# Weight loads of a four-stage hybrid decoder layer issued from GpSimd's queue instead of SyncE's

## The chip, the cores and the metric

One core of a Trainium2 chip runs the whole kernel in one launch. The metric is the device time of one execution in microseconds (us); lower is better. The engines are named as the profile names them: PE (TensorE, matmuls), PEld (TensorE's weight loads), DVE (VectorE), ACT (ScalarE), POOL (GpSimd), SP (SyncE, which here only issues DMAs; its rows are marked SPq).

## The reference, cut to what matters

One layer of a decoder is applied to 1024 prompt tokens and to 8 x 4 sample tokens, 1056 tokens in all, everything in float32:

```
h = rmsnorm(x);  z = h @ w_in                       # 1024 -> 6432 columns
u = z_c[:512] * sigmoid(z_c[512:]);  c = silu(layernorm(dwconv31(u)));  ya = c @ w_conv_out
r,k,v,decay,alr,gate = token-shifted z_r (+ small LoRA products)
S_t = S_{t-1} diag(w_t) + (S_{t-1} a_t) b_t^T + v_t k_t^T;  y_t = S_t r_t       # 16 heads of 64
yb = groupnorm(y) ... @ w_rw_out
x = x + (sig(g1)*ya + sig(g2)*yb) @ w_mix_out
up = rmsnorm(x) @ w_up;  f = gelu(dwconv3(up)[:3072]) * dwconv3(up)[3072:];  x = x + f @ w_down
```

The outputs are the two normalised results and the new states.

## The kernel before, in words

**Weights.** Every large product is done as three matmuls in a reduced float format (`mm3`, L69 to L73): the high part of the weights with the high part of the activations, the high part with the low part, and the low part with the high part. So each weight tile is split before use, in `wjob` (L41 to L51), `wjob2` (L1572 to L1582) and `ffn_last` (L1589 to L1595), always in three steps: a DMA brings the tile `wraw` (L47, L1579, L1593; 128 partitions with up to 8 runs of 512 bytes each, 512 KB), ACT rounds it to `whi` (L48), and POOL subtracts to get `wlo` (L49). There are 155 such loads. `wraw` has one buffer up to the end of the convolution's output product (pool `wraw`, L110) and two after that (pool `wraw2`, L120); `whi` and `wlo` have two each (L108). A new load may start when the `wlo` of the load before has been computed, since that is the last reader of the buffer; the next `whi` may be written when the product that used the buffer two tiles ago is done.

**Stages.** The work goes through five stretches. (1) Start (to about 63 us): nine token tiles are loaded, normalised and transposed into `hH` and `hL`; parameter rows are loaded (`consts`, L158 to L170) and transposed (`turn`, L172). (2) Convolution (to about 317 us): products for the gated convolution input and for the LoRA inputs, while DVE does 31 taps per channel tile (L359). (3) Recurrence (to about 1395 us, `mixer_b`): 16 blocks of 256 tokens go through `prep` (L885), `stage` (L992), `combine` (L1061), `chain` (L1089) and `group_norm` (L1159), and the remaining products of `w_in` (`rkv_tile`, `gate`) are woven between as filler. In `prep` POOL builds `BK` (L982, L983) and scales `alr` (L957). In `stage` POOL masks `LQ` and `E` (L1011), SP stores and reloads pieces of `LQ` (L1019, L1021), DVE inverts small triangles (L1028, L1030), and the result goes out and back (L1034, L1038). The order of these streams is written by a small planner (`drive`, L701) that keeps its own matmul clock; it knows nothing of DMAs. (4) Convolution output (to about 1458 us): `conv_out` (L432), per tile one half-size weight load, a load of `ga` (L438), a product of 36 matmuls and a store `d_ma` (L443); at the same time 1 MB pieces of the recurrence's result are loaded into `hL` (L819). (5) Tail (to the end): `merge`, `mix`, and the gated MLP (`ffn_up`, `ffn_down`, `ffn_last`), 72 or 54 matmuls per weight tile.

**Queues.** All DMAs go through SP's queue in order, but for eight small parameter rows that POOL issues in `consts` (L168, groups 1 to 3). An instruction that waits at the head of a queue holds all behind it. Within each engine a scheduler orders the instructions from the order in which the code emits them and from its own estimate of their durations.

Of the kernel before, what the change touches and what calls it, by code (L numbers as in the profile page):

```python
# [31 lines left out]
class Net:  # L32
# [8 lines left out]
    def wjob(self, src, nk=8, lo_eng=None):  # L41
        nc = self.nc
        m = src.shape[-1]
        raw = self.rp.tile([128, 8, 128], F32, tag="wraw", name="wraw")
        hi = self.wp.tile([128, 8, 128], F32R, tag="whi", name="whi")
        lo = self.wp.tile([128, 8, 128], F32R, tag="wlo", name="wlo")
        nc.sync.dma_start(out=raw[:, :nk, :m], in_=src.rearrange("(k p) c -> p k c", p=128))  # L47
        nc.scalar.activation(out=hi[:, :nk, :m], in_=raw[:, :nk, :m], func=AF.Copy)  # L48
        (lo_eng or nc.gpsimd).tensor_tensor(  # L49
            out=lo[:, :nk, :m], in0=raw[:, :nk, :m], in1=hi[:, :nk, :m].bitcast(F32), op=ALU.subtract)  # L50
        return hi, lo  # L51
# [1520 lines left out]
    def wjob2(self, src, nk, lo_eng=None):  # L1572
        nc = self.nc
        m = src.shape[-1]
        v = lambda t: t.rearrange("p a b -> p (a b)")[:, :nk * m].rearrange("p (k c) -> p k c", c=m)
        raw = v(self.rp.tile([128, 8, 128], F32, tag="wraw", name="wraw"))
        hi = v(self.wp.tile([128, 8, 128], F32R, tag="whi", name="whi"))
        lo = v(self.wp.tile([128, 8, 128], F32R, tag="wlo", name="wlo"))
        nc.sync.dma_start(out=raw, in_=src.rearrange("(k p) c -> p k c", p=128))  # L1579
        nc.scalar.activation(out=hi, in_=raw, func=AF.Copy)  # L1580
        (lo_eng or nc.gpsimd).tensor_tensor(out=lo, in0=raw, in1=hi.bitcast(F32), op=ALU.subtract)
        return hi, lo  # L1582

    def ffn_last(self, g, f, acc, room):

        nc, a, G = self.nc, self.a, self.G
        rows = a["w_down"][0][g * G * 128:(g + 1) * G * 128]
        wh, wl = (t[:, 0:G, 0:D] for t in room)
        for h in range(4):  # L1589
            raw = self.rp.tile([128, 8, 128], F32, tag="wraw", name="wraw")  # L1590
            raw = raw.rearrange("p a b -> p (a b)")[:, :G * 256].rearrange("p (k c) -> p k c", c=256)
            c = slice(h * 256, (h + 1) * 256)
            nc.sync.dma_start(out=raw, in_=rows[:, c].rearrange("(k p) c -> p k c", p=128))  # L1593
            nc.scalar.activation(out=wh[:, :, c], in_=raw, func=AF.Copy)
            nc.gpsimd.tensor_tensor(out=wl[:, :, c], in0=raw, in1=wh[:, :, c].bitcast(F32), op=ALU.subtract)  # L1595
        with ExitStack() as e:
            xp = self.pool(e, "fin", 2)
            last = None
            for t0, t1 in ((0, 3), (3, 6), (6, 9)):
                toks = self.TOK[t0:t1]  # L1600
                c0 = toks[0][0]
                w = sum(n for _, n in toks)
                s = slice(c0, c0 + w)
                ssum = xp.tile([128, 384], F32, tag="ssum", name="ssum")
                for i in range(ND):
                    c = slice(i * 128, (i + 1) * 128)
                    ps = self.pm.tile([128, 512], F32, tag="mm", name="mm")
                    for k in range(G):
                        self.mm3(ps[:, :w], (wh[:, k, c], wl[:, k, c]), (f[k][0][:, s], f[k][1][:, s]), k == 0, k == G - 1)
                    x = acc[i][:, s]  # L1610
                    nc.vector.tensor_tensor(out=x, in0=ps[:, :w], in1=x, op=ALU.add)
                    if i == 0:
                        nc.scalar.activation(out=ssum[:, :w], in_=x, func=AF.Square)
                    else:
                        sq = xp.tile([128, 384], F32, tag="sq", name="sq")
                        nc.scalar.activation(out=sq[:, :w], in_=x, func=AF.Square)
                        nc.gpsimd.tensor_tensor(out=ssum[:, :w], in0=ssum[:, :w], in1=sq[:, :w], op=ALU.add)
                    nc.scalar.activation(out=x, in_=x, func=AF.Copy, scale=self.col("norm_final_g", i))
                    if last and i % 2:
                        next(last, None)  # L1620
                last = self.final(xp, acc, toks, ssum)
            self.run(last)
# [59 lines left out]
```

## Time and profile before

| | us |
|---|---|
| median of 3 runs | 2564.65 |
| lowest, highest of 3 runs | 2553.85, 2574.9 |
| the profiled execution | 2538.03 |
| its span, from the first to the last instruction | 2536.3 |

The profile is of one execution, with every instruction's start and length. Busy time is the time in which an engine ran at least one instruction. A wait is the idle time of an engine just before an instruction, put down to what released it. The granted clock is the rate at which PE was allowed to run, as a share of full speed. The chain of work that ended last is followed back from the last instruction. A DMA's own row on SP or POOL is the time of its issue, not of its transfer.

### The profile page before, as it was taken

The numbers are of one execution on the slowest core, as the hardware profiler recorded it, in microseconds if no ns is written. First come the engines' busy times: TensorE is split into PE (matmuls) and PEld (weight loads), VectorE is DVE, ScalarE is ACT, GpSimd is POOL, SyncE is SP. The second block draws the span as 40 slices with busy tenths as digits, with TensorE's granted clock in tenths as the row PEclk, the third lists the DMA queues.
The fourth block names the chain that finished last, engine by engine and source line by source line (L and its number), as shares of the span: only waits on it lengthen the run. The fifth ranks groups of instructions, "written<-read, shape, count | busy, mean of one in ns | idle before, by whom it ended". The sixth has DMA issues, their size and how long they took to land.

```text
span 2536.3 us, 41660 instructions
## 1 busy us (share of the span) xinstructions
PE 2367.6 (93%) x16094; PEld 2140.9 (84%) x16094; DVE 1427.9 (56%) x3588; ACT 918.7 (36%) x1748; POOL 909.1 (36%) x879
## 2 busy tenths in 40 slices
PE   5889989999788799999989999999999999999998
PEld 4878888777676677777777899999999999999998
DVE  5799955586646674555464434465444534445345
ACT  4133433354244354454434322333222222223125
POOL 3332253244324443443333243433323323323333
PEclk9899987898688698999779999999999999999999
DMA  3223443243233333533323854431111111111111
GB/s 104 56 60 130 171 149 89 81 121 93 78 89 79 93 107 83 140 98 94 94 64 96 273 178 131 128 128 44 44 47 48 44 51 44 47 48 41 54 46 75
DMA packets 307640, 230.64 MB, mean 91 GB/s; under 512 B 90492, under 2 KB 287123, under 8 KB 306921
## 3 DMA queue, kind: packets, MB, share of 16 engines
q1 hardware_dynamic: 307185, 227.80, 31.1%
q8 instruction: 127, 2.08, 0.4%
q14 instruction: 72, 0.59, 0.1%
q0 software_dynamic: 256, 0.17, 0.0%
HBM read 157.45 MB, written 70.45 MB: 90 GB/s over the span
## 4 chain that ended last, share of the span: by engine, by line
PE 66%; DVE 7%; DMA 7%; POOL 3%; issue 2%; ACT 1%; SPq 1%; POOLq 0%; DVEq 0%; ACTq 0%
PE mm L54 52%; PE w L54 7%; DMA L<-dL 4%; PE c L54 2%; PE y L54 2%; PE w L61 2%; DVE tm L1028 1%; DVE x L1030 1%; DVE t L961 1%; DMA ga<-d_ga 0%; POOL BK L982 0%; POOL wlo L49 0%; POOL LQ L1011 0%; DVE lnQ L666 0%; DVE v L486 0%
## 5 line engine op out<-in xcount | busy, mean ns | idle before, releaser
L54 PE MATMUL mm<-hH,whi 128*128 128x352 f32 (+1 forms) x2568 | 887.6, 346 | 27.0 <-DVE bcol L496 11.2
L54 PE MATMUL mm<-hL,whi 128*128 128x352 f32 (+1 forms) x2568 | 866.2, 337 | 0.2 <-DVE hL L248 0.2
L54 PE MATMUL mm<-hH,wlo 128*128 128x352 f32 (+1 forms) x2568 | 862.7, 336 | 0.0
L54 PEld LDWEIGHTS mm<-hH,whi 128*128 128x128 f32 (+1 forms) x2568 | 499.4, 194 | 55.9 <-issue 14.1
L54 PEld LDWEIGHTS mm<-hL,whi 128*128 128x128 f32 (+1 forms) x2568 | 500.9, 195 | 11.2 <-DVE hL L248 0.5
L54 PEld LDWEIGHTS mm<-hH,wlo 128*128 128x128 f32 (+1 forms) x2568 | 500.6, 195 | 8.7 <-issue 0.2
L49 POOL TENSOR_TENSOR wlo<-wraw,whi 128x1024 fp32r<-128x1024 f32 (+2 forms) x123 | 292.5, 2378 | 462.0 <-ACT whi L48 427.9
L48 ACT ACTIVATE whi<-wraw 128x1024 fp32r<-128x1024 f32 (+2 forms) x123 | 126.0, 1025 | 366.8 <-PE mm L54 270.1
L1544 DVE SCALAR_TENSOR_TENSOR c<-u,par,c 128x1024 f32<-128x1024 f32 x96 | 167.0, 1739 | 55.6 <-ACT c L1540 55.6
L359 DVE SCALAR_TENSOR_TENSOR sg<-cu,par,sg 128x1024 f32<-128x1024 f32 x120 | 185.1, 1550 | 3.4 <-ACT sg L357 1.7
L1514 DVE TENSOR_TENSOR u<-mm,rs 128x352 f32<-128x352 f32 x144 | 73.2, 509 | 186.5 <-PE mm L54 186.3
L54 PE MATMUL mm<-fH,whi 128*128 128x352 f32 x504 | 163.4, 324 | 0.0
L1569 DVE TENSOR_TENSOR acc<-mm,acc 128x352 f32<-128x352 f32 x168 | 86.8, 523 | 135.0 <-PE mm L54 135.0
L54 PE MATMUL mm<-fH,wlo 128*128 128x352 f32 x504 | 162.7, 323 | 0.0
L54 PE MATMUL mm<-fL,whi 128*128 128x352 f32 x504 | 162.7, 323 | 0.0
L1028 DVE TENSOR_TENSOR tm<-L,x 128x60 f32<-128x60 f32 (+24 forms) x496 | 99.4, 200 | 79.7 <-DMA L<-dL 72.5
L1030 DVE TENSOR_TENSOR x<-x,tm 128x60 f32<-128x60 f32 (+24 forms) x496 | 105.0, 212 | 7.0
L1525 POOL COPY lr<-u 128x2 f32<-128x2 f32 x48 | 9.0, 187 | 276.3 <-DVE u L1514 267.6
L54 PE MATMUL w<-E,BK 64*128 64x128 f32 x512 | 90.7, 337 | 8.8 <-DVE tm L1028 3.4
L1011 POOL TENSOR_SCALAR_AFFINE_SELECT LQ<-LQ 64x512 f32<-64x512 f32 x64 | 44.1, 690 | 148.3 <-ACT LQ L1007 146.8
L54 PEld LDWEIGHTS mm<-fH,whi 128*128 128x128 f32 x504 | 94.8, 188 | 0.5
L54 PEld LDWEIGHTS mm<-fH,wlo 128*128 128x128 f32 x504 | 95.0, 188 | 0.0
(379 smaller groups left out, 3971.2 us busy)
## 6 DMA issues: line engine op xcount, KB each, us to landing
wraw<-w_in SPq DMA_DIRECT2D x50, 512.0 KB
wraw<-w_up SPq DMA_DIRECT2D x48, 512.0 KB
wraw<-w_down SPq DMA_DIRECT2D x32, 384.0 KB
L<-dL SPq DMA_DIRECT2D x16, 512.0 KB
d_alr<-la SPq DMA_DIRECT2D x8, 528.0 KB
d_cum<-lc SPq DMA_DIRECT2D x8, 528.0 KB
d_gout<-lg SPq DMA_DIRECT2D x8, 528.0 KB
d_k<-k SPq DMA_DIRECT2D x8, 528.0 KB
```

The source lines that it names most:

```text
L48: nc.scalar.activation(out=hi[:, :nk, :m], in_=raw[:, :nk, :m], func=AF.Copy)
L49: (lo_eng or nc.gpsimd).tensor_tensor(out=lo[:, :nk, :m], in0=raw[:, :nk, :m], in1=hi[:, :nk, :m].bitcast(F32), op=ALU.subtract)
L54: self.nc.tensor.matmul(out, l, r, start=start, stop=stop)
L61: self.nc.tensor.transpose(out, x, ident)
L359: nc.vector.scalar_tensor_tensor(out=c[:, 0:TP], in0=u[:, t:t + TP], scalar=self.col("conv_w", t * 4 + i), in1=c[:, 0:TP], op0=ALU.mult, o ...
L961: nc.vector.scalar_tensor_tensor(out=t1[:, u], in0=r[:, u], scalar=self.col("r_k", 2 * J + u), in1=km[:, u], op0=ALU.mult, op1=ALU.mult)
L1011: nc.gpsimd.affine_select(out=w, in_=w, pattern=[[0, 4], [1, 2], [1, 64]], compare_op=ALU.is_ge, fill=0.0, base=-1, channel_multiplier=-1)
L1028: nc.vector.tensor_tensor(out=tm[:, :a, :m], in0=L[:, s:s + 1, s + 1:32].to_broadcast([128, a, m]), in1=X[:, :a, s:s + 1].to_broadcast([12 ...
L1030: nc.vector.tensor_tensor(out=X[:, :a, s + 1:32], in0=X[:, :a, s + 1:32], in1=tm[:, :a, :m], op=ALU.add)
L1514: nc.vector.tensor_tensor(out=u[:, 2 + t0:2 + t0 + m], in0=p, in1=rs[:, t0:t0 + m], op=ALU.mult)
L1544: nc.vector.scalar_tensor_tensor(out=c[:, 0:TP], in0=u[:, t:t + TP], scalar=wt, in1=c[:, 0:TP], op0=ALU.mult, op1=ALU.add)
L1569: nc.vector.tensor_tensor(out=acc[i][:, s], in0=ps[:, :BW], in1=acc[i][:, s], op=ALU.add)
```

## The change

The three statements that load weights are issued from POOL's queue in place of SP's; nothing else is edited.

```diff
@@ wjob @@
-        nc.sync.dma_start(out=raw[:, :nk, :m], in_=src.rearrange("(k p) c -> p k c", p=128))
+        nc.gpsimd.dma_start(out=raw[:, :nk, :m], in_=src.rearrange("(k p) c -> p k c", p=128))
@@ wjob2 @@
-        nc.sync.dma_start(out=raw, in_=src.rearrange("(k p) c -> p k c", p=128))
+        nc.gpsimd.dma_start(out=raw, in_=src.rearrange("(k p) c -> p k c", p=128))
@@ ffn_last @@
-            nc.sync.dma_start(out=raw, in_=rows[:, c].rearrange("(k p) c -> p k c", p=128))
+            nc.gpsimd.dma_start(out=raw, in_=rows[:, c].rearrange("(k p) c -> p k c", p=128))
```

All 155 loads move, and the scheduler orders the other instructions somewhat differently around them. On POOL at the start, where the first load stands at the head of the queue, this is the difference (+ is the changed kernel):

```order
+L49 TENSOR_TENSOR wlo<-wraw,whi 128x1024
 L165 MEMSET st 128x128
 L168 DMA st<-conv_dw_w 124x128
-L128 ISA
-L128 AFFINE_SELECT ident<-ident 128x128
 L168 DMA st<-conv_dw_b 4x128
 L168 DMA st<-conv_ln_g 4x128
 L168 DMA st<-conv_ln_b 4x128
-L49 TENSOR_TENSOR wlo<-wraw,whi 128x1024
 L168 DMA st<-ffn_dw_b 48x128
 L168 DMA st<-ffn_dw_w 48x128 x3
+L47 DMA wraw<-w_in 128x8x128
```

The first `wlo` now stands ahead of the memset of the parameter tile `st` and of POOL's parameter loads, and the second weight load stands behind them.

On POOL where the recurrence begins (the first `prep`: `P`, `PC`, `BK` and `alr` are its tiles), before:

```order
L49 TENSOR_TENSOR wlo<-wraw,whi 128x1024 x2
L903 MEMSET P 128x8
L906 COPY PC<-P 128x8
L982 TENSOR_TENSOR BK<-kn,cum 64x8x64 x2
L49 TENSOR_TENSOR wlo<-wraw,whi 128x1024
L957 TENSOR_TENSOR alr<-alr,k 128x512
L983 TENSOR_TENSOR BK<-alr,cum 64x8x64 x2
```

and in the changed kernel, same engine and place:

```order
L49 TENSOR_TENSOR wlo<-wraw,whi 128x1024
L47 DMA wraw<-w_in 128x8x128
L49 TENSOR_TENSOR wlo<-wraw,whi 128x1024
L47 DMA wraw<-w_in 128x8x128
L903 MEMSET P 128x8
L906 COPY PC<-P 128x8
L982 TENSOR_TENSOR BK<-kn,cum 64x8x64 x2
L49 TENSOR_TENSOR wlo<-wraw,whi 128x1024
L957 TENSOR_TENSOR alr<-alr,k 128x512
L47 DMA wraw<-w_in 128x8x128
L983 TENSOR_TENSOR BK<-alr,cum 64x8x64 x2
```

Each load follows the `wlo` that frees its buffer, here between `alr` and the second pair of `BK`. In the whole recurrence 8 loads stand right ahead of a mask of L1011 and 2 right ahead of a `BK`.

On SP in the convolution output (`hL` are the 1 MB pieces of the recurrence's result, `d_ma` the stores of the stage's product), the difference:

```order
-L47 DMA wraw<-w_conv_out 128x4x128
 L819 DMA hL<-d_y_426 128x2112
+L819 DMA hL<-d_y_427 128x2112
 L443 DMA d_ma_401<-ga 128x1056
-L47 DMA wraw<-w_conv_out 128x4x128
-L819 DMA hL<-d_y_427 128x2112
+L819 DMA hL<-d_y_428 128x2112
+L443 DMA d_ma_402<-ga 128x1056
 L438 DMA ga<-d_ga_411 128x1056
```

The weight loads are gone from between the `hL` loads, and the third `hL` load now stands ahead of the first `d_ma` store.

## Rows read from the trace of the kernel before

**Rows 1.** The page: busy time, share of the span and instructions of PE and POOL, and the granted clock of PE in 40 equal slices (tenths).
```profile
PE 2367.6 (93%) x16094; PEld 2140.9 (84%) x16094; DVE 1427.9 (56%) x3588; ACT 918.7 (36%) x1748; POOL 909.1 (36%) x879
...
PEclk9899987898688698999779999999999999999999
```

**Rows 2.** Busy time of each engine by stage (start, convolution, recurrence, convolution output, tail): stretch, its length, then per engine the busy us and instructions, then the granted clock, the DMA engines' share and GB/s.
```profile
0.00:63.40 63.40, 35.24 (x181) 27.24 (x182) 34.48 (x107) 29.36 (x50) 19.40 (x47) 0.92 0.34 104
63.40:317.00 253.60, 235.44 (x1283) 208.38 (x1283) 234.49 (x234) 87.80 (x151) 78.46 (x48) 0.95 0.32 104
317.00:1395.00 1078.00, 970.04 (x7620) 799.51 (x7619) 634.46 (x2379) 471.73 (x1068) 423.88 (x443) 0.85 0.37 97
1395.00:1458.40 63.40, 57.33 (x357) 55.15 (x358) 28.64 (x50) 23.49 (x33) 16.00 (x12) 0.97 0.84 273
1458.40:2536.30 1077.90, 1069.52 (x6663) 1050.66 (x6661) 495.81 (x818) 306.33 (x446) 371.37 (x331) 1.00 0.23 70
```

**Rows 3.** The page: the chain of work that ended last, share of the span by engine (a q marks an engine's queue, issuing or waiting).
```profile
PE 66%; DVE 7%; DMA 7%; POOL 3%; issue 2%; ACT 1%; SPq 1%; POOLq 0%; DVEq 0%; ACTq 0%
```

**Rows 4.** What SP's queue waited for, whole span: instruction, releaser, us in total, times, longest.
```profile
SPq L47 <- POOL wlo L49: 531.9, 81, 17.9
```

**Rows 5.** The same for the recurrence alone (317 to 1395 us).
```profile
SPq L47 <- POOL wlo L49: 60.9, 13, 10.5
...
SPq L47 <- POOL PC L906: 11.5, 2, 10.9
```

**Rows 6.** The DMA issues of line L168, on POOL: count, then duration in ns, least, median and most.
```profile
L168 POOL DMA_DIRECT2D st<-ffn_dw_w x3: 667/672/810, 12.9 to 14.3; - x3
...
L168 POOL DMA_DIRECT2D st<-conv_dw_w x1: 729/729/729, 1.4 to 1.4; - x1
L168 POOL DMA_DIRECT2D st<-conv_dw_b x1: 562/562/562, 2.4 to 2.4; - x1
```

**Rows 7.** The issues of line L47 on SP, same columns.
```profile
L47 SPq DMA_DIRECT2D wraw<-w_in x51: 367/396/1454, 2.2 to 1353.5; - x51
```

**Rows 8.** The timeline of the start: start us, length us, instruction, and in brackets the idle time before it with its releaser.
```profile
4.30 1.06 ACT L230 ACTIVATE jk<-xt 128x1024 f32<-128x1024 f32 x1 [2.21 <-DMA xt<-x_prompt]
...
8.91 1.06 ACT L48 ACTIVATE whi<-wraw 128x1024 fp32r<-128x1024 f32 x1 [0.54 <-DMA wraw<-w_in]
...
10.05 2.34 POOL L49 TENSOR_TENSOR wlo<-wraw,whi 128x1024 fp32r<-128x1024 f32 x1 [6.07 <-ACT whi L48]
...
15.02 0.21 POOL L631 TENSOR_SCALAR_AFFINE_SELECT mrow<-mrow 32x8 f32<-32x8 f32 x1
...
21.06 1.42 POOL L646 TENSOR_SCALAR_AFFINE_SELECT x<-x 32x256 f32<-32x256 f32 x3
22.51 0.43 DVE L1025 COPY x<-x 128x256 f32<-128x256 f32 x1 [7.59 <-POOL x L646]
22.84 0.26 DVE L179 COPY par<-w 128x107 f32<-128x107 f32 x1
...
23.83 0.66 PE L54 MATMUL mm<-hH,whi 128*128 128x352 f32 x1
```

**Rows 9.** POOL's groups by line in the recurrence: count, busy us, mean ns, then the idle time just before them and its releasers.
```profile
L49 POOL TENSOR_TENSOR wlo<-wraw,whi 128x1024 fp32r<-128x1024 f32 x34 | 82.2, 2417 | 149.5 <-ACT whi L48 135.7 <-DMA dL<-LQ 9.0 <-PE mm L54 2.5
L1011 POOL TENSOR_SCALAR_AFFINE_SELECT LQ<-LQ 64x512 f32<-64x512 f32 x64 | 44.1, 690 | 148.3 <-ACT LQ L1007 146.8 <-DVE rt L664 1.2
```

**Rows 10.** From the chain of work in the recurrence, single pieces: start us, length us, what.
```profile
351.35 2.37 POOL wlo L49
353.71 1.70 POOL alr L957
...
495.12 0.28 SPq L47
```

**Rows 11.** In the convolution output: SP's timeline (start us, length us, instruction).
```profile
1407.42 0.42 SPq L47 DMA_DIRECT2D wraw<-w_conv_out  x1
...
1421.57 0.32 SPq L443 DMA_DIRECT2D d_ma<-ga  x1
1426.69 0.38 SPq L47 DMA_DIRECT2D wraw<-w_conv_out  x1
1427.17 0.46 SPq L819 DMA_DIRECT2D hL<-d_y  x1
...
1453.06 0.39 SPq L47 DMA_DIRECT2D wraw<-w_conv_out  x1
```

**Rows 12.** The same stage: what PE waited for from 1400 to 1470 us, in the columns of Rows 4.
```profile
PE mm L54 <- DVE ga L441: 4.9, 3, 3.6
```

**Rows 13.** The same stage, the stretches 1400 to 1430 and 1430 to 1445 us, in the columns of Rows 2.
```profile
1400.00:1430.00 30.00, 28.83 (x181) 28.25 (x180) 13.93 (x25) 14.78 (x21) 9.47 (x7) 1.00 0.90 292
1430.00:1445.00 15.00, 10.23 (x52) 9.39 (x50) 8.16 (x11) 5.38 (x6) 2.56 (x2) 0.89 0.91 325
```

**Rows 14.** In the tail (1650 to 2450 us): what ACT waited for before it wrote `whi`, in the columns of Rows 4.
```profile
ACT whi L48 <- PE mm L54: 148.0, 34, 7.9
```

**Rows 15.** POOL's group of L49 in the convolution (126.8 to 317 us), in the columns of Rows 9.
```profile
L49 POOL TENSOR_TENSOR wlo<-wraw,whi 128x1024 fp32r<-128x1024 f32 x10 | 27.5, 2747 | 89.2 <-ACT whi L48 73.4 <-PE w L596 15.7
```

## The prediction

> **What bounds the kernel now.** I read the busy times first, then the table by stage, then the chain and the waits of single queues. PE is busy 93% of the span, and its granted clock is full in the last 23 or so of 40 slices and lower in many of the first 22 [rows 1]. The table by stage says where time could be won at all [rows 2]. In the tail PE is busy 1069.5 of 1077.9 us at full clock: nothing that is done to DMAs can shorten it. In the recurrence PE is busy 970 of 1078 us at a mean clock of 0.85, so about 108 us of idle PE and some slow clock are on offer. In the convolution DVE is busy 234.5 of 253.6 us and sets the pace. In the chain of work, PE has 66%, DMA 7%, POOL 3% and SP's queue 1%, which is about 25 us of 2536 [rows 3].
>
> The queue that the change relieves looks bad at first sight: SP waits 532 us at L47 for POOL's `wlo` [rows 4], and everything behind a waiting load is held. But this wait lies mostly where nobody needs SP. Inside the recurrence it is 60.9 + 11.5 = 72 us [rows 5], and the piece of L47 that I find on the chain of work there is 0.28 us long [rows 10]. Nor are the weights late: in the tail ACT waits 148 us for PE to give back a `whi` buffer [rows 14], which means that the next tile was lying ready.
>
> **The price of one load on POOL.** No load of this size is issued from POOL before. The nearest rows are the parameter loads: 0.56 us for 4 rows, 0.67 for 48, 0.73 for 124 rows of 512 bytes [rows 6]. A weight load has 128 x 8 = 1024 such runs. If runs cost nothing the price is 0.73 us. From 4 to 124 rows it grows by (729 - 562)/120 = 1.4 ns per row, which would make 0.56 + 1.4 = 2.0 us; from 4 to 48 rows by (672 - 562)/44 = 2.5 ns, which would make 3.1 us. I take 1.3 us, between the 124-row load itself and its own line, and keep 0.7 and 3.1 as ends. On SP the issue cost 0.4 us [rows 7], so SP saves 155 x 0.4 = 62 us of issue, and POOL gains 155 x 1.3 = 200 us: from 909 to 1110 us, 44% of the span. POOL is far from full; what counts is what stands behind a load.
>
> **Stage by stage.** *Start.* Before, POOL runs without a gap from the first `wlo` at 10.05 us to the masks' end at 22.5 us; DVE's copy L1025 waits for these, the parameters' copy L179 stands behind it on DVE, and the first product starts at 23.83 us [rows 8]. After, the first load stands at the head of POOL's queue and no longer behind three token tiles, so `whi` can be written about when the first tile's square is done (4.30 + 1.06 us and a transfer shared with the tiles): I estimate 6.5 us, `wlo` at 7.6 us. Behind it POOL has 2.3 us of `wlo`, the memset, 5.0 us of parameter loads (0.73 + 0.56 + two of about 0.5 + 0.55 + 2.14), the second weight load at 1.3 us and the masks, 15.02 to 22.48 us, 7.5 us: 16.3 us, so L1025 at 23.9 us, 1.4 us later than now. SP's parameter loads must wait for that memset, now behind `wlo`; they would land near 16 us and stay hidden under the masks. In return the squares of tiles 3 to 6 are done during the wait. Net +1 us; ends: -3 (all of that ACT work gained back) and +6 (`wlo` as late as now, load at 3.1 us).
>
> *Convolution.* 14 loads, DVE bound, `wlo` waits for ACT and not the reverse [rows 15]: 0, ends -3 and +3.
>
> *Recurrence.* 34 loads [rows 9], 34 x 1.3 = 44 us more on a POOL that is busy 424 of 1078 us. Ten loads stand right ahead of a mask or a `BK`. That place matters: before, a `wlo` of 2.37 us followed by `alr` is on the chain [rows 10], and the load now stands right behind that `alr`, ahead of `BK`. But POOL waits 146.8 us for ACT ahead of the masks [rows 9], so about half of these loads fall into idle time: 5 x 1.3 = 6.5 us on the stage chain, of which filler products hide about half: +3 us; ends 0 and 10 x 3.1 = 31 us. Against it SP is freed: 34 x 0.4 us of issue and 72 us of waiting. On the chain I saw 0.28 us of it; I take -2 us. The end is all that SP's queue has on the chain, -25 us. Net +1 us.
>
> *Convolution output.* Here the transfers themselves are the limit: the DMA engines are busy 0.90 and 0.91 of the time at 292 and 325 GB/s [rows 13], and PE lost 15 - 10.23 = 4.8 us, put down to `ga` [rows 12, 13]. One tile's loads follow each other by (1453.06 - 1407.42)/6 = 7.6 us [rows 11]. After, the load starts without SP, but costs 1.3 - 0.4 = 0.9 us more in each of six rounds. More important is the order on SP. Now the weight load's wait at the head of SP, until 1426.69 us, holds back the next 1 MB `hL` load to 1427.17 us [rows 11]: the wait paces the big loads. After, three `hL` loads go ahead of the first `d_ma` store, whose landing lets the next `ga` load start. At 300 GB/s a megabyte is 3.5 us, so the store and the `ga` behind it come some 3.5 us later, once or twice, and PE waits more at L441. Sum +5 us; ends -5 (PE's loss given back) and +14 (two megabytes and six times 0.9 us, rounded up).
>
> The Trainium skill ("DMA: Bandwidth & Descriptors", section Issuing engines are not separate DMA queues) says that all issuers share the same DMA engines, and that several issuers save only the sequencer's time. By that rule the change could win only the 0.4 us issues and the waits ahead of them; the DMA share of 0.9 in this stage agrees, and the sum would be as above without any gain here.
>
> *Tail.* 96 loads, PE always busy, tiles ready ahead [rows 2, 14]; POOL goes from 371 to 371 + 125 of 1078 us: 0, ends 0 and +2. Should that cover be gone (a load later than a product's 11.7 us), PE would wait; POOL's sum per tile leaves room for that even at 3.1 us.
>
> The sum is 1 + 0 + 1 + 5 + 0 = +7 us: 2538 + 7 = 2545 us for an execution like the profiled one. This ran 26.6 us under the median of the runs, which share everything but PE's clock; so I add the 7 us to the median: 2564.65 + 7 = 2572 us. All ends together give -36 and +56 us.
>
> **Rivals.** *SP's relief is real.* SP has 1% of the chain [rows 3], and a load that waits at its head may also hold the small transfers of `stage`, which the chain books as DMA. If the whole 25 us go and conv output gives its 4.8 us back, the time is 2565 - 30 = 2535 us. For it: 72 us of waits in the recurrence [rows 5]. Against: only one piece on the chain is a load's. It decides if the transfers L1019 to L1038 start earlier by over 1 us per block.
>
> *POOL becomes what the recurrence waits for.* One mechanism: the load's descriptor work stands ahead of `BK` and the masks, and each `stage` starts later by it. From about 2.5 us per load on it outweighs everything else: 10 x 3.1 = 31 us, with 5 to 14 us in the convolution output and 2 more at the start about +38 us, 2603 us. For it: ten loads stand exactly there, and the blocks follow one another. Against: POOL idles for ACT ahead of the masks [rows 9], and 4 or 124 rows cost nearly the same [rows 6].
>
> The Trainium skill ("SBUF — State Buffer", section SBUF: two separate sides) adds that GpSimd cannot write descriptors while DVE runs in a two-port mode. By it each load could also be held by one DVE operation, some 0.3 us on average here (634 us over 2379 instructions), 10 us over 34 loads. The trace so far shows little of it: beside the busiest DVE `wlo` takes 2747 ns against 2417 ns in the recurrence [rows 9, 15].
>
> *Nothing starts earlier.* With one `wraw` buffer a load cannot start before the last `wlo` in either queue, so weights come no sooner: 2565 us, within the forecast's band.
>
> **How the numbers follow.** Forecast 0.50; relief 0.18; POOL as the bound 0.26; nothing moves 0.06. About 1%, 25.6 us, is what a measurement of this kernel can tell from no change. Faster by over 1% is the relief alone, 0.18; slower by over 1% the POOL case, 0.26; the rest, 0.56, is within 1%. The range takes in the relief's 2535 us and reaches past the POOL case to 2615 us, near the sum of the ends (2529 and 2621 us) with little cut off. The forecast's own range is 2550 to 2590 us.
>
> **What would show it.** Right, if POOL's load rows last 0.7 to 2 us, POOL is busy near 1100 us, SP shows no wait at L47, the tail is 1078 us long within 2 us, the start's first product comes at 24 to 26 us, and PE waits more for `ga` around 1430 us. Wrong, if load rows last over 3 us, if PE waits for `wlo` or `whi` anywhere, or if the recurrence is over 25 us shorter or longer with the same clock.

## The result, and the profile after

| | before | changed | ratio, 95% interval |
|---|---|---|---|
| first measurement, median of 4 and 4 runs | 2559.25 us | 2576.98 us | 1.0104 [1.0056, 1.0152] |
| repeated on one chip, median of 23 and 12 runs | 2558.31 us | 2575.90 us | 1.0048 [1.0012, 1.0085] |
| the profiled executions | 2538.03 us | 2568.93 us | |

The changed kernel is slower, by about 18 us between the medians both times (by 12 us, 0.48%, in the repeated ratio); the forecast was 2572 us, 7 us slower than before. The ratios leave out runs over 1.5% above the kernel's own fastest, which here are the upper end of one continuous spread, so medians of all runs stand beside them in this text.

The page of the changed kernel, in the columns of [rows 1]:

```profile
PE 2374.9 (93%) x16094; PEld 2146.3 (84%) x16094; DVE 1442.8 (56%) x3588; ACT 917.8 (36%) x1748; POOL 1035.8 (40%) x1034
...
PEclk9999987888788789798779899999999999999999
```

POOL has its 155 loads more (879 and 155 are 1034 instructions) and is 127 us busier, not 200. The busy times by stage, against [rows 2]; I moved the later cuts by as much as an event near each moved (the last `sg` of the convolution by 1.0 us, the first and the last L441 of the convolution output by 23.4 and 29.7 us):

```profile
0.00:64.10 64.10, 31.79 (x181) 26.04 (x182) 32.30 (x107) 30.93 (x51) 24.20 (x52) 0.98 0.36 111
64.10:318.00 253.90, 236.12 (x1303) 210.19 (x1303) 237.49 (x236) 87.97 (x152) 84.82 (x63) 0.96 0.31 103
318.00:1418.40 1100.40, 980.37 (x7623) 803.85 (x7622) 647.22 (x2383) 469.26 (x1067) 452.29 (x476) 0.84 0.36 95
1418.40:1488.10 69.70, 56.16 (x329) 54.95 (x328) 29.04 (x46) 23.15 (x33) 21.16 (x19) 0.90 0.71 246
1488.10:2567.20 1079.10, 1070.48 (x6665) 1051.31 (x6663) 496.74 (x818) 306.53 (x446) 453.30 (x427) 1.00 0.23 70
```

The lengths differ from before by +0.7, +0.3, +22.4, +6.3 and +1.2 us, 30.9 in all. In the recurrence PE is idle 1100.4 - 980.4 = 120.0 us where it was 1078.0 - 970.0 = 108.0; the other 10 us are PE busy for longer, at a granted clock of 0.84 for 0.85. So about half of the largest piece is waiting and half goes with the clock, and the clock differs from run to run: one pair of profiles can't settle this stage. The experiments had to.

*The loads.* Line, engine, operation, count; then least, median and most duration in ns:

```profile
L47 POOL DMA_DIRECT2D wraw<-w_in x51: 889/917/1031, 1.3 to 1365.2; - x51
...
L47 POOL DMA_DIRECT2D wraw<-w_conv_out x8: 754/759/789, 1394.7 to 1483.7; - x8
```

A load costs 0.92 us on POOL where [rows 7] has 0.40 on SP; with half the runs (`w_conv_out`) it is 0.76.

*The start.* The timeline of the changed kernel, against [rows 8]:

```profile
0.82 3.40 SPq L203 DMA_DIRECT2D xt<-x_prompt  x7
...
1.34 1.03 POOL L47 DMA_DIRECT2D wraw<-w_in  x1 [0.82 <-POOLq L1670]
...
10.58 1.06 ACT L48 ACTIVATE whi<-wraw 128x1024 fp32r<-128x1024 f32 x1 [5.23 <-DMA wraw<-w_in]
...
11.72 2.36 POOL L49 TENSOR_TENSOR wlo<-wraw,whi 128x1024 fp32r<-128x1024 f32 x1 [8.95 <-ACT whi L48]
...
28.53 0.43 DVE L1025 COPY x<-x 128x256 f32<-128x256 f32 x1 [5.54 <-POOL x L646]
...
29.85 0.66 PE L54 MATMUL mm<-hH,whi 128*128 128x352 f32 x1
```

The load is issued first, at 1.34 us, and yet its tile is split at 10.58 us, later than the 8.91 of before: SP, with no weight load between, now issues seven token tiles in a row (it was three), and all share the DMA engines, which are busy for 0.83 of the first 10.5 us (before: 0.65). ACT waits 5.23 us for the load with the token tiles' squares behind it, POOL waits 8.95 us with the parameters and masks behind it, and the first product starts at 29.85 us, 6.0 later.

*The convolution output.* SP's timeline, against [rows 11], and then what PE waited for in it, against [rows 12]:

```profile
1437.94 0.55 SPq L819 DMA_DIRECT2D hL<-d_y  x1
...
1439.63 0.92 SPq L819 DMA_DIRECT2D hL<-d_y  x2
1448.52 0.32 SPq L443 DMA_DIRECT2D d_ma<-ga  x1
1448.93 0.38 SPq L819 DMA_DIRECT2D hL<-d_y  x1
1453.86 0.32 SPq L443 DMA_DIRECT2D d_ma<-ga  x1
1454.23 0.42 SPq L438 DMA_DIRECT2D ga<-d_ga  x1
```

```profile
PE mm L54 <- DVE ga L441: 11.7, 3, 10.2
```

Three megabytes of `hL` go out before the first `d_ma` store, and the third `ga` load comes some 14 us after the third `hL`. Before, it came 1428.84 - 1427.17 = 1.7 us after it:

```profile
1428.84 0.32 SPq L438 DMA_DIRECT2D ga<-d_ga  x1
```

PE's wait for `ga` grows from 4.9 to 11.7 us, 10.2 of it in one piece.

*SP in the recurrence.* What SP's queue waited for, against [rows 5], here of the stretch 317 to 1395 us again:

```profile
SPq L1019 <- POOL LQ L1011: 122.1, 25, 19.0
SPq L1199 <- ACT y L1191: 45.0, 8, 8.7
SPq L455 <- ACT gt L454: 44.6, 6, 15.7
```

No wait at L47 is left. But SP did not become free: the store of a gate (L455), behind which it waited little before, now holds it for 44.6 us. Before, that row and the first were:

```profile
SPq L1019 <- POOL LQ L1011: 116.9, 23, 19.0
...
SPq L455 <- ACT gt L454: 13.6, 3, 12.1
```

SP's wait for POOL's masks (L1011) is nearly the same, 122.1 for 116.9 us, and 115.2 in rec_only below, which moves the loads of this stage alone. What shrank is POOL's own wait for ACT ahead of the masks, which was 146.8 us [rows 9]:

```profile
POOL LQ L1011 <- ACT LQ L1007: 104.4, 39, 14.0
```

So the loads went largely into time in which POOL had been waiting.

### The profile page after: what moved, and what is told of

Its sections match the earlier page's. It is cut to its first block, busy times and chain, and to the rows that moved or that the text cites. A ratio compares the mean times of both kernels' runs of the same rounds, so it can differ in the third digit from the quotient of the medians.

```text
span 2567.2 us, 41576 instructions
## 1 busy us (share of the span) xinstructions
PE 2374.9 (93%) x16094; PEld 2146.3 (84%) x16094; DVE 1442.8 (56%) x3588; ACT 917.8 (36%) x1748; POOL 1035.8 (40%) x1034
## 2 busy tenths in 40 slices
DMA packets 191703, 230.63 MB, mean 90 GB/s; under 512 B 89468, under 2 KB 152979, under 8 KB 190985
## 3 DMA queue, kind: packets, MB, share of 16 engines
q0 software_dynamic: 20944, 74.76, 10.3%
## 4 chain that ended last, share of the span: by engine, by line
PE 64%; DMA 7%; DVE 6%; POOL 3%; ACT 2%; issue 2%; SPq 1%; ACTq 0%; POOLq 0%; DVEq 0%
PE mm L54 50%; PE w L54 6%; DMA L<-dL 4%; PE c L54 2%; PE y L54 2%; PE w L61 2%; DVE tm L1028 1%; DVE t L961 1%; DVE x L1030 1%; POOL BK L982 1%; DMA wraw<-w_conv_out 0%; DMA dX<-X 0%; DMA sl<-state_wkv 0%; DMA st<-state_ffn 0%; POOL alr L957 0%
## 5 line engine op out<-in xcount | busy, mean ns | idle before, releaser
L54 PE MATMUL mm<-hH,whi 128*128 128x352 f32 (+1 forms) x2568 | 885.1, 345 | 23.0 <-DVE bcol L496 10.5
L49 POOL TENSOR_TENSOR wlo<-wraw,whi 128x1024 fp32r<-128x1024 f32 (+2 forms) x123 | 291.2, 2368 | 435.3 <-ACT whi L48 376.2
L48 ACT ACTIVATE whi<-wraw 128x1024 fp32r<-128x1024 f32 (+2 forms) x123 | 126.0, 1025 | 366.2 <-PE mm L54 276.1
L1028 DVE TENSOR_TENSOR tm<-L,x 128x60 f32<-128x60 f32 (+24 forms) x496 | 98.9, 199 | 91.4 <-DMA L<-dL 84.6
L54 PEld LDWEIGHTS w<-E,BK 64*128 64x128 f32 x512 | 77.9, 236 | 24.0 <-issue 13.0
```

The costliest lines, as they stand in the source:

```text
L49: (lo_eng or nc.gpsimd).tensor_tensor(out=lo[:, :nk, :m], in0=raw[:, :nk, :m], in1=hi[:, :nk, :m].bitcast(F32), op=ALU.subtract)
L54: self.nc.tensor.matmul(out, l, r, start=start, stop=stop)
L1028: nc.vector.tensor_tensor(out=tm[:, :a, :m], in0=L[:, s:s + 1, s + 1:32].to_broadcast([128, a, m]), in1=X[:, :a, s:s + 1].to_broadcast([12 ...
```

## The experiments

In all of them the loads that aren't named stay on SP (in no_rec they go to POOL). PE's idle time is counted from the first L1028 (the first triangular solve) to the first L441, as the length of that window less PE's busy time. Before has 100.9 us there:

```profile
390.50:1416.90 1026.40, 925.52 (x7415) 758.22 (x7415) 605.97 (x2326) 453.64 (x1033) 392.84 (x407) 0.85 0.37 96
```

The changed kernel has 111.7 us:

```profile
387.40:1440.30 1052.90, 941.23 (x7412) 769.53 (x7411) 618.80 (x2324) 452.73 (x1033) 421.25 (x438) 0.84 0.36 94
```

**rec_only, the recurrence's 34 loads on POOL.**

```diff
@@ gate, rkv_tile (from its third j on) @@
-    self.wjob(self.a["w_in"][0][:, c0:c0 + 128])
+    self.wjob(self.a["w_in"][0][:, c0:c0 + 128], q=self.nc.gpsimd)
@@ wjob @@
-    nc.sync.dma_start(out=raw[:, :nk, :m], ...)
+    (q or self.nc.sync).dma_start(out=raw[:, :nk, :m], ...)
```

> Only the 34 loads of the recurrence go to POOL, the other 121 stay on SP. Theory 1 (what stands behind a load on POOL is late, some 20 us in the recurrence): +18 to +24 us against before, the last mask of L1011 15 to 25 us later, the convolution output as before (51.8 us from the first to the last L441). Theory 2 (the two profiled runs differ in the recurrence by the clock's own spread, the load costs +1 us): within 6 us of before. Theory 3 (loads on a second queue contend with the recurrence's transfers): +18 to +24 us as well, with L<-dL taking longer than before.

**no_rec, the complement:** the same edit with the queues exchanged.

> The complement: the 34 loads of the recurrence stay on SP, the other 121 go to POOL. All theories: first product near 29.9 us, given back by 60 us; convolution output 5 to 7 us longer with the longest wait of PE for ga near 10 us; tail +0 to +2. Theories 1 and 3: +6 to +9 us in all, and together with the run above +25 to +32. Theory 2: +6 to +9 us, and together with the run above at most +15, short of the +18 measured between the medians.

Measured: rec_only 2570.01 against 2561.47 us, 1.0037 [1.0002, 1.0071]; no_rec 2562.25, 1.0011 [0.9979, 1.0042]. The window of rec_only, then that of no_rec:

```profile
387.40:1444.30 1056.90, 945.67 (x7415) 771.72 (x7414) 620.16 (x2324) 452.96 (x1034) 418.26 (x437) 0.84 0.35 94
```

```profile
385.90:1432.70 1046.80, 949.98 (x7424) 776.97 (x7425) 606.04 (x2326) 453.45 (x1033) 398.53 (x412) 0.83 0.36 94
```

PE is idle 111.2 us in rec_only and 96.8 in no_rec. So the recurrence's loads carry most of the loss. The 8.5 us between the medians are less than theories 1 and 3 gave; at equal clock (last section) it is 17 us, just under their band. Theory 2's 6 us lie inside the interval; what speaks against them is that figure and the idle time. The last mask comes 20 us later, as theory 1 had it, but 24 us later in conv_only too, where the recurrence's loads stay on SP, so this sign tells nothing. Theory 3 falls by the transfers themselves: from its issue to the first operation that uses it, `L<-dL` takes 176.8 us in sum over the 16 blocks in rec_only and 174.7 before. no_rec keeps the start's delay (first turn of a token tile into `hH` at 28.5 us for 23.2), which is gone by the convolution's end (last `sg` at 308.0 us for 309.4). Its convolution output is 3.6 us longer where 5 to 7 were expected, and PE's longest wait for `ga` is 3.9 us where 10 were.

**conv_only, the 8 loads of `w_conv_out` on POOL** (`q=self.nc.gpsimd` in `conv_out` alone).

> Only the 8 loads of w_conv_out go to POOL. If the order on SP (the third hL load ahead of the first d_ma store) makes the convolution output longer: +5 to +7 us from the first to the last L441, PE's longest wait for ga about 10 us, start and tail as before. If it is the loads' own later landing: +1 to +3 us, with PE waiting for whi or wlo instead.

Measured: 2558.81 us, 1.0007 [0.9972, 1.0043]; the stage lasts 55.4 us from first to last L441 for 51.8 before, and SP again sends three `hL` ahead of the first `d_ma`:

```profile
PE mm L54 <- DVE ga L441: 6.8, 2, 4.3
```

PE waits for `ga` and for no `whi` or `wlo`, as the theory of SP's order says; the +3.6 us are less than it gave, and too little to show in the time. The stage depends on how it is reached as well: with these loads on SP it lasts 50.8 to 52.7 us in most kernels below, but 54.5 in rec_act and 59.2 in rec_4x; the changed kernel's two profiles have 58.1 and 59.9 us. This profile also shows how much the clock does by itself. Its recurrence has its loads on SP as before, and yet it took 36 us longer than before's, at a granted clock of 0.82, with less idle time (97.5 us):

```profile
386.30:1448.50 1062.20, 964.67 (x7434) 791.14 (x7434) 607.29 (x2327) 455.35 (x1038) 400.64 (x414) 0.82 0.35 93
```

**rec_act, the recurrence's loads on ACT's queue** (`q=self.nc.scalar`).

> The 34 loads of the recurrence go to ACT's queue, the other 121 stay on SP. Theory 1 (POOL's order): the loads no longer stand ahead of BK and the masks, so within 6 us of before. Theory 2 (spread): within 6 us too. Theory 3 (a second queue contends with L<-dL): +18 to +24 us, as on POOL. ACT's own queue may be held by a load that waits for wlo; if that counts, ACT shows waits for POOL at L47 of over 30 us in all and the time rises by a like share of it.

Measured: 2554.70 against 2561.47 us, 0.998 [0.9947, 1.0013], no difference that can be told. In time that is nearest to theories 1 and 2, and theory 3's +18 us is out. But PE's idle time is 111.7 us, as with POOL; the time doesn't show it, since these runs had the highest clock of all (0.9245 in the middle, before 0.917). So a queue other than POOL's goes with the same idle time. It doesn't clear POOL, though, for here ACT was held: 26 of the 34 loads were issued 0.03 us after the `wlo` that they had waited for, and ACT stood for up to 50 us in all ahead of its loads.

**after_again, the changed kernel once more.**

> The changed kernel once more, beside the kernel before on one chip. If the stages add up (recurrence loads +0.37%, the rest +0.11%), 1.003 to 1.008 of before, some +8 to +20 us, with PE idle for 108 to 115 us between the first product of the first triangular solve (L1028) and the first L441 where before has 97 to 101, the convolution output 55 to 59 us long, and tail and start as in its first profile. If the first result (1.0104) stands, 1.009 to 1.012, and the parts don't add up.

Measured: 1.0048 [1.0012, 1.0085], idle 106.7 us, convolution output 59.9 us. Idle time is a little under its band and the convolution output a little over; the ratio is that of the sum of the parts (0.37% and 0.11%), and the median 17.6 us over before.

**rec_4x, each of the recurrence's loads as four DMAs on POOL.**

```diff
@@ wjob, for a load with q @@
-    q.dma_start(out=raw[:, :nk, :m], ...)
+    for k in (0, 2, 4, 6):
+        q.dma_start(out=raw[:, k:k + 2, :m], ...)
```

> Like rec_only, but each of the 34 loads of the recurrence is issued on POOL as four DMAs of two row blocks each. Theory POOL time (the issue's time on POOL ahead of stage work is what costs): POOL is busy 34 x 3 x 0.7 = 70 us longer, PE's idle time in the recurrence rises from 111 to 130 us or more, the time is 15 to 40 us over rec_only. Theory interleave (the moved loads only change the order in which the products of the recurrence and of the projections alternate on PE; POOL has room): PE's idle time 100 to 120 us, the time within 12 us of rec_only in either direction.

Measured: 2595.42 us, 1.0104 [1.0039, 1.0168], 25 us over rec_only by the medians; idle 121.7 us. A quarter costs 0.72 us, so a load holds POOL for 2.9 us:

```profile
L47 POOL DMA_DIRECT2D wraw<-w_in x136: 720/720/792, 306.3 to 1375.1; - x136
```

Its size lies between the two theories' bands in idle time, and in the time, of four runs, it is what theory POOL time gave. But its order differs from rec_only's, too, and the last two runs show what that alone can do.

**rec_memset, POOL's time without the move.** The loads stay on SP; POOL writes the tile full of zeros in the place where the load would stand, and the load waits for that.

```diff
@@ wjob, for the recurrence's loads @@
+    nc.gpsimd.memset(raw[:, :nk, :m], 0.0)
     nc.sync.dma_start(out=raw[:, :nk, :m], ...)
```

> All loads on SP as before; ahead of each of the 34 loads of the recurrence POOL writes zeros over the wraw tile, about 1 us on POOL in the place where the load stands after the change. Theory POOL time: the cost of rec_only without the move of the queue, PE idle 108 to 115 us, +6 to +14 us against before. Theory interleave: the cost follows the order that comes out; POOL's extra 34 to 40 us by themselves are hidden, PE idle within 95 to 105 us and the time within 6 us of before, unless the order moves as well, which the rows of order would show as other stretches of PE idle than in rec_only.

Measured: 34 writes of 0.95 us; 0.9986 [0.9943, 1.003], but the median of all 12 runs is 2566.73 against 2558.31 us, since four of them lie above 2586 us, at clocks of 0.898 to 0.908. Idle 105.9 us. By these numbers neither theory is told from the other. At equal clock (last section) this kernel is 3 us slower than before: POOL held as long as by the loads costs little in this order.

**rec_st_act and st_act, SP's new wait taken away.** With the loads gone from SP, gate stores hold it (L455 above), and in rec_only the issue of `L<-dL` comes 164.1 us in sum after the last `dL` store, 145.4 before. In rec_st_act the stores L455 and L464 go to ACT's queue besides the loads to POOL, in st_act alone.

```diff
@@ gate, rkv_tile @@
-    nc.sync.dma_start(out=dst, in_=g[:, :T])
+    nc.scalar.dma_start(out=dst, in_=g[:, :T])
...
-    nc.sync.dma_start(out=self.d_rkv[n][j // 2][:, j % 2], in_=t)
+    nc.scalar.dma_start(out=self.d_rkv[n][j // 2][:, j % 2], in_=t)
```

> rec_only (the 34 loads of the recurrence on POOL), and the stores of the gates (L455) and of the projections (L464) go from SP to ACT's queue. Theory head of SP (without the loads SP runs ahead into a store whose tile is not ready, and the load L<-dL behind it is late): the delay from the last dL store to the issue of L<-dL falls from 164 us in sum to 150 or less, PE's idle time in the recurrence from 111 to 95 to 104 us, the time to within 5 us of before. Theory interleave (the order of products on PE that comes with the moved loads costs by itself, whatever SP waits for): PE idle 108 to 116 us and +6 to +14 us against before.

> All loads on SP as before; only the stores L455 and L464 go to ACT's queue. Theory head of SP: the waits of SP for these stores' tiles are gone, PE idle 90 to 100 us, 0 to 10 us faster than before. Theory interleave: the order moves here too, PE idle 105 to 115 us, +3 to +14 us against before.

Measured: rec_st_act 1.0115 [1.0062, 1.0167], idle 107.5 us; st_act 1.0099 [1.0067, 1.0132], idle 108.3 us. The delay of `L<-dL` did fall, to 143.7 and 136.5 us, and the time rose all the same. So taking the late `L<-dL` away won nothing, as the theory of SP's head had it. But the wait did not vanish: ACT now stands for about 39 us in each of the two kernels at the stores of L464, and what that costs was not told from the cost of the order.

**rec_tiny and rec_tiny_dve, another order for next to nothing.** As rec_memset, but only one column (128 x 1) is written, by POOL or by DVE; the load waits for it.

```diff
@@ wjob, for the recurrence's loads @@
+    nc.gpsimd.memset(raw[:, 0, 0:1], 0.0)      # rec_tiny_dve: nc.vector
     nc.sync.dma_start(out=raw[:, :nk, :m], ...)
```

> All loads and stores on SP as before; ahead of each of the 34 loads of the recurrence POOL writes one column of zeros (128 x 1) into the wraw tile, about 0.1 us each, 3 us in all, no descriptors and nothing on a second queue. The order of all engines in the recurrence moves as it does in rec_only. Theory interleave (any other order than the one of before costs PE idle time in the recurrence): PE idle 104 to 116 us where before's order has 97 to 101; the time +3 to +20 us. Theory load on POOL (the issue of the load or the transfer from a second queue is what costs): PE idle 96 to 102 us, the time within 5 us of before.

> The same with the one column written by VectorE in place of POOL, so a third order of the recurrence with next to no work added (34 x about 0.06 us on DVE). Theory interleave: PE idle 104 to 116 us again, the time +3 to +20 us. Theory load on POOL: PE idle 96 to 102 us, the time within 5 us of before. One of the two kernels near before and one not would say that an order may be as good as the one of before by luck.

On PE, this is the first place where rec_tiny's order leaves before's (`mm` are the projections' products, `w` those of a block's matrices; + is rec_tiny):

```
+L54 MATMUL mm<-hH,whi 128x352
 L54 MATMUL w<-t_2859,bones 128x512
 L54 MATMUL w<-E_2861,BK 128x128 x4
 L54 MATMUL w<-E_2862,BK 128x128 x4
-L54 MATMUL mm<-hH,whi 128x352
```

One product of a projection has moved ahead of a block's products; by an alignment of the two traces some 1800 of the 16094 products stand in another place, and some 4200 in rec_tiny_dve. In no_rec and conv_only it is about 150, nearly all of them after 1379 us, so these two have before's order in nearly the whole recurrence. Measured: rec_tiny 2570.69 against 2559.94 us, 1.0049 [1.0018, 1.008]; rec_tiny_dve 2599.91 us, 1.0164 [1.0118, 1.021]. The added writes, of rec_tiny and then of rec_tiny_dve:

```profile
L47 POOL MEMSET wraw<- x34: 92/99/104, 305.4 to 1377.0; 128x1 f32 x34
```

```profile
L47 DVE MEMSET wraw<- x34: 59/59/59, 309.4 to 1403.7; 128x1 f32 x34
```

And their windows in the same order:

```profile
394.20:1446.10 1051.90, 944.38 (x7416) 774.34 (x7415) 615.50 (x2325) 453.25 (x1033) 395.69 (x437) 0.83 0.36 94
```

```profile
383.90:1461.60 1077.70, 965.49 (x7424) 787.38 (x7424) 611.19 (x2357) 456.63 (x1038) 400.31 (x412) 0.82 0.35 93
```

With 3.4 and 2.0 us of added work, off PE, PE is idle 107.5 and 112.2 us, and the ratio is above rec_only's. The theory of the interleave gave that, though rec_tiny_dve's +40 us lie over its band of +3 to +20; the theory of the load on POOL gave 96 to 102 us and no change in time. The loads did not come much later for the write ahead of them: ACT waits 27.8 and 27.6 us in all for loads at L48, before 24.9. In rec_tiny_dve, DVE also waits 5.3 us for `wlo` at its write, so rec_tiny is the cleaner of the two.

## Why the prediction was right, and where it was not

- **The price of a load:** 1.3 us was taken, 0.92 measured, inside the ends; 155 loads make 135 us of issue and POOL is 1036 us busy, where I gave 1110. The line through 4, 48 and 124 rows overstated what 1024 runs cost.
- **The clock's row:** it is full in the last 19 slices of [rows 1], not in 23; no term hangs on this.
- **Start:** the sum held (+1 forecast; +0.7 at the stage's end), the step did not. I had `whi` at 6.5 us and the first product at 24 to 26; it was 10.58 and 29.85. I moved the load to the head of POOL's queue and forgot what its leaving does to SP: seven token tiles go out at once and share the DMA engines with it. The loss of 6 us was given back behind it, since the squares were already done and DVE sets the pace there.
- **Convolution:** 0 forecast, +0.3 measured.
- **Recurrence:** this is the term that was mis-sized, "Net +1 us". It was worked out as POOL time ahead of `BK` and masks (+3) against SP's relief (-2). Measured, the 34 loads cost 8.5 us between the medians (0.37%, 0.02 to 0.71) and 17 at equal clock. The loads fell largely into POOL's idle time (the sum had about half), and SP's wait for the masks did not grow, so the traces show no sign of the first mechanism. Runs with before's order in this stage (before, no_rec, conv_only) have 97 to 101 us of idle PE; all nine kernels in which anything moved its order have 106 to 122, whether the loads went to POOL or ACT, stores went to ACT, or one column was written. The term left out is that the change reorders the products on PE between the blocks and the projections: rec_tiny shows that a new order with next to no work costs 0.49%, 8 us at equal clock, and rec_tiny_dve has 19. That it makes up all of the 17 us is not shown. I had read the rows of order only on POOL and SP.
- **SP's relief:** as forecast (-2 us), it is worth next to nothing: no run shows a gain from it. SP's 60.9 us at L47 turned into waits at the next transfers in line, L455 above all.
- **Convolution output:** +5 forecast, +6.3 measured (8.1 in the second profile, 3.6 with these loads alone and in no_rec), by the mechanism named: a third `hL` ahead of the first `d_ma`, and PE waiting at L441, though at 1460 us and not at 1430 (the stage began 23 us later). The 3.6 us come with these loads; the rest may come with the order in which the stage is reached, for rec_4x has +7.4 us with these loads on SP.
- **Tail:** 0 to +2 forecast, +1.2 measured.
- **PE's waits for weights,** which were to be a sign against the forecast: none in the changed kernel's first profile, 0.6 us in its second, and 0.4 us before.
- **The rivals.** *SP's relief is real* is out. *POOL becomes the bound* set in, if at all, at 2.9 us per load (rec_4x), the point that I gave as 2.5; how much of that run's loss is its order stays open. That DVE's operations hold up a load on POOL shows in none of its issue rows: the longest of the 51 of `w_in` took 1.03 us, 0.11 over the median. The Trainium skill's rule that all issuers share the same DMA engines ("DMA: Bandwidth & Descriptors", section Issuing engines are not separate DMA queues) agrees with the start, where the load from a second queue still came late (its tile was split at 10.58 us for 8.91).

So the range and the sign were right, and the +7 us came from the right stage only for the convolution output; the larger part arose in the recurrence, where the sum had +1. That the 2572 us lie within 5 us of the measured medians is in part luck: before itself came out 5 us faster than in the three runs that I had added to, and the changed kernel ran at a higher clock, which hid a part of its loss. What stays open: how much of the recurrence's loss is the order and how much the loads on POOL. But for rec_4x, the kernels with loads on POOL lie among those without in idle time, and a kernel that moves the loads and holds the order was not tried.

## What to carry to other kernels

Where a scheduler places the instructions, moving one kind of them to another queue is two changes: the one that was written, and a new order of everything around it. Run a control that moves the order and costs next to nothing, as one column written here, before a difference of 1% is put down to a queue. And a wait at the head of a queue is worth only what stands behind it: taken away, it is replaced by the next instruction that isn't ready, and a queue that was held back may then send its large transfers too early.

## What was not expected of the hardware

The time of this kernel is a matter of the clock's mean to a degree that I had not seen in one profile: over 92 timed runs of the kernel before, from 2538.64 us at a mean granted clock of 0.923 to 2591.05 at 0.903, a straight line of 2.15 us per 0.001 fits with 3.2 us left over. By that line the changed kernel's 12 repeated runs lie 26 us above before at equal clock, and its clock in the middle was 0.921 for 0.917, which gives some 9 us back: the idle time that the change adds does not arrive in full. The other kernels follow nearly the same slope (1.85 to 2.46 us per 0.001 in the ten with six runs or more), so the line can be used to compare all of them. Mean distance of the runs from it, in us, each with a standard error of 1 to 3:

| kernel | above before at equal clock |
|---|---|
| the changed kernel, repeated | 26 |
| rec_only; no_rec; conv_only | 17; 7; 2 |
| rec_act | 12 |
| rec_4x | 31 |
| rec_memset | 3 |
| rec_st_act; st_act | 22; 22 |
| rec_tiny; rec_tiny_dve | 8; 19 |

This sorts the kernels better than the medians do. rec_only and no_rec make 24 of the 26 us, so the recurrence's loads are two thirds of the loss. Equal idle time is not equal loss: rec_memset and rec_tiny have 106 and 108 us of it and lose 3 and 8 us, st_act has 108 and loses 22. A new order with next to no work cost 8 us in rec_tiny and 19 in rec_tiny_dve, and POOL's time without the move cost 3 in rec_memset. So an order can cost as much as rec_only's 17 us; that its order makes up all of them is not shown.

That PE's idle time raises the mean clock is not shown, and st_act speaks against it: more idle time than before, and a lower clock (0.9145 in the middle). Why one order gets a higher clock than another stays open.

The changed kernel moved its bytes in fewer packets. From its page, the queue that SP uses and the one that POOL uses:

```profile
q1 hardware_dynamic: 170561, 153.21, 20.3%
q0 software_dynamic: 20944, 74.76, 10.3%
```

The columns are packets, MB and the packets' share of 16 engines' time. The weights go at 74.76 MB / 20944 = 3.6 KB a packet, and the whole kernel has 191703 packets for 307640 before. The share of time is nearly unchanged, 30.6% for 31.1%, so the DMA engines gained little by it.
